# Where a unit of weights begins in its tile: one start per stage and block instead of two

## The chip, the cores and the metric

The kernel runs on one core of a Trainium2 chip. The metric is the device time of one execution in microseconds (us); lower is better. The kernel before was timed twice: 2617.41 and 2624.41 us, median 2620.91 us.

## What is computed

One decoder layer in float32, with 512 rows of 2048 numbers. Cut to its products:

```python
q_a, k_a, v_a, q_b, k_b, v_b = split(h @ w_in)            # 2048 -> 4608 columns
o_a = swa_sink_attention(q_a, k_a, v_a, sinks)            # 16 heads, window of 128
o_b = stick_breaking_attention(q_b, k_b, v_b)             # 16 heads
h = layer_norm(ALPHA * h + concat(rms(o_a), rms(o_b)) @ w_o)
h = layer_norm(ALPHA * h + memory_cross_attention(h, mem, w_q, w_kv, w_o_mem))
gate, up = split(h @ w_gate_up)                           # 2048 -> 2 x 5632
h = layer_norm(ALPHA * h + (silu(gate) * up) @ w_down)    # 5632 -> 2048
```

## The kernel before

All weights go through TensorE in units of 128 x 1024 float32 numbers. For each unit SyncE loads the raw numbers into a staging tile (`stage`, line 137), ScalarE casts them to a rounded half `hi` (line 131), and VectorE subtracts that from the raw numbers and writes the rest as a second half `lo` (line 132). Activations are held as such pairs too. A product is then three matmuls (`mm3`, lines 157 to 162, and its forms for the feed-forward part, `product` at line 1074 and `product_turned` at line 1085): hi by hi, hi by lo, lo by hi. Each matmul comes with a weight load of 128 columns, since TensorE holds one operand (the stationary one, 128 x 128) and streams the other (the moving one) in 256 or 512 columns.

Both halves of a unit lie in one tile of 2048 + 16 float32 numbers, 8256 bytes per partition (`weight_pair`, line 143). Three such tiles are used in turn. The argument `shift` says at which number of the tile `hi` begins; `lo` begins 1024 numbers later. Before the change there are two values: 0, and `SHIFT` = 16 numbers, that is 64 bytes. The three tiles and all tiles of activations that the products below read begin 32 bytes past a multiple of 128 bytes. So a unit with shift 0 begins 32 bytes past such a multiple, and one with shift 16 begins 96 bytes past it.

The stages in order of time. Counts are matmuls on units of weights:

| units | what | operand that the weights are | columns streamed | matmuls | shift before |
|---|---|---|---|---|---|
| wvb | values of B | moving | 512 | 384 | 0 |
| wva | values of A | moving | 256 | 192 | 0 |
| wkb, wqb, wka, wqa | projections, between pieces of attention | stationary | 512 | not touched | 0 |
| wmv, wmk | values and keys of the memory | stationary | 256 | 768 each | 16 |
| wo, wmo | output projections | moving | 512 | 768, 384 | 0 |
| wmq | queries of the memory, turned into `kq` | stationary | 256 | 768 | 16 |
| wvo | mixed values | moving | 512 | 384 | 0 |
| wge | parts of gate and up ahead of time | stationary | 256 | 576 | 16 |
| gu3, gu0, gu4, gu1, gu5, gu2, gu6 to gu10 | gate and up, in this order | stationary | 256 | 672 each; gu0, gu1, gu2: 480 | 16 |
| dn0_0, dn0_1, dn1_0, dn1_1, dn2_0, dn2_1 | down | moving | 512 | 336 each; dn2_0, dn2_1: 252 | 0 |

The order on TensorE and SyncE is written out by hand; the other engines take their work in an order that a scheduler sets when the program is built. TensorE waits for a unit's `hi` (from ScalarE) and `lo` (from VectorE), and ScalarE waits for TensorE to be done with the tile three units earlier. In the gate and up blocks VectorE also adds two raw tiles for most units (line 620), which with line 132 makes two passes over 1024 numbers a unit.

In traces a unit has its name without numbers that count buffers: `gu7w`, `wmk_0w`, `dn_0w` (all units of dn0_0, dn1_0 and dn2_0), `wva2w`.

Of the kernel before, what the change touches and what calls it, by code (L numbers as in the profile page):

```python
# [64 lines left out]
def layer(ctx, tc, io, out):  # L65
# [72 lines left out]
    def stage(src, name):  # L138
        st = pw.tile([P, 1024], F32, tag="ws", name=f"{name}s")
        nc.sync.dma_start(st, src)  # L140
        return st

    def weight_pair(name, shift=0):

        pair_pools.append(pair_pools.pop(0))
        w = pair_pools[-1].tile([P, 2048 + SHIFT], F32R, tag="w", name=f"{name}w")
        return [w[:, k * 1024 + shift:][:, :1024] for k in range(2)]

    def unit(src, name, shift=0):
        st = stage(src, name)  # L150
        hi, lo = weight_pair(name, shift)
        latest[0] = split(hi, lo, st).ins
        return hi, lo
# [57 lines left out]
    for nb in range(2):  # L211
        acc = four_banks(nb, f"v{nb}")
        for u in range(8):
            if nb == 0 and u == 0:
                st, ws = pw.tile([P, 2, 512], F32, tag="ws", name="x0s"), pw.tile([P, 1024], F32, tag="ws", name="wvb0s")
                w = weight_pair("wvb0")
                for c in range(2):
                    nc.sync.dma_start(st[:, c], io["xT"][0][:, cs(c, 512)])
                    nc.sync.dma_start(ws[:, cs(c, 512)], io["w_vb"][0, 0][:, cs(c, 512)])
                for c in range(2):  # L220
                    split(*xc(c), st[:, c])
                    split(*at(w, ALL, cs(c, 512)), ws[:, cs(c, 512)])
            elif nb == 0:
                st = stage(io["xT"][u], f"x{u}").rearrange("p (c n) -> p c n", c=2)
                for c in range(2):
                    split(*xc(2 * u + c), st[:, c])
            if nb > 0 or u > 0:
                w = unit(io["w_vb"][nb, u], f"wvb{nb}_{u}")
            for c in range(2):
                for t in range(NT):  # L230
                    mm3(acc[t], at(xc(2 * u + c), ALL, cs(t, P)), at(w, ALL, cs(c, 512)),
                        u == 0 and c == 0, u == 7 and c == 1)
        for t in range(NT):
            split(vb[t][0][:, cs(nb, 512)], vb[t][1][:, cs(nb, 512)], acc[t])
    load_consts()
    acc = four_banks(0, "va")
    for u in range(4):
        w = unit(io["w_va"][u], f"wva{u}")
# [354 lines left out]
    def steps(name, src, groups, partial, last):  # L593
# [19 lines left out]
        def hilo(src_):  # L613
            hi, lo = weight_pair(name, shift)
            latest[0] = split(hi, lo, src_).ins
            latest[1] = casts[-1]
            return hi, lo
# [93 lines left out]
    def next_unit():  # L711
        while len(ahead) <= AHEAD:
            w = next(source, None)
            if w is None:
                break
            ahead.append(w)
        return ahead.pop(0)
# [18 lines left out]
    for nb in range(4):  # L736
        acc = four_banks(nb, f"wo{nb}")
        for u in range(8):
            w = next_unit()
# [107 lines left out]
    for h in range(4):  # L847
        for nb in range(4):
            acc = ps_z(f"vo{nb}_{h}")
            for u in range(2):  # L850
                w = next_unit()
# [176 lines left out]
    for half in range(2):  # L1028
        for pair in range(2):
            acc = four_banks(1 - pair, f"pvo{half}_{pair}")  # L1030
            spare[:] = [ps_tr, ps_av, ps_lin, ps_lin] if pair == 1 else [ps_z1]
            for h in range(4):
                for j in range(2):
                    nb = 2 * pair + j
                    w = next_unit()
# [324 lines left out]
    for i, kind in enumerate(block_kinds):  # L1360
# [15 lines left out]
        for place in order:  # L1376
            name, role = PRODUCTS[place]
# [109 lines left out]
```

## Time and profile before

| | |
|---|---|
| two timed runs | 2617.41 and 2624.41 us, median 2620.91 us |
| the profiled execution | 2628.31 us |
| its span, first to last instruction | 2626.4 us |
| TensorE matmul busy | 97% of the span |
| TensorE weight loads busy | 87% |
| VectorE, ScalarE, GpSimd busy | 73%, 45%, 7% |
| granted TensorE clock, mean | 0.993 |

PE is TensorE's matmuls, PEld its weight loads, DVE is VectorE, ACT is ScalarE, POOL is GpSimd. Matmuls overlap: a row gives one matmul from its start to its end, which is longer than the distance to the next one's start. That distance is read from a stretch of time and the count of matmuls in it. A count includes those that reach over the edges of the stretch, about two at these lengths.

### The profile page before, as it was taken

The numbers are of one execution on the slowest core, as the hardware profiler recorded it, in microseconds if no ns is written. First come the engines' busy times: TensorE is split into PE (matmuls) and PEld (weight loads), VectorE is DVE, ScalarE is ACT, GpSimd is POOL, SyncE is SP. The second block draws the span as 40 slices with busy tenths as digits, with TensorE's granted clock in tenths as the row PEclk, the third lists the DMA queues.
The fourth block names the chain that finished last, engine by engine and source line by source line (L and its number), as shares of the span: only waits on it lengthen the run. The fifth ranks groups of instructions, "written<-read, shape, count | busy, mean of one in ns | idle before, by whom it ended". The sixth has DMA issues, their size and how long they took to land.

```text
span 2626.4 us, 40562 instructions
## 1 busy us (share of the span) xinstructions
PE 2555.2 (97%) x16544; PEld 2294.9 (87%) x16544; DVE 1907.0 (73%) x2183; ACT 1189.8 (45%) x1572; POOL 186.9 (7%) x325
## 2 busy tenths in 40 slices
PE   9999999999999999999999999999999998999996
PEld 7887777799988889988999999999999997878874
DVE  4258888997632474447788888888887778777797
ACT  4246566665521254334554444544455443333332
POOL 0001101110000000000100101010111001000001
PEclk9999999999999999999999999999999999999998
DMA  5322222245752484235755656464555577787765
GB/s 184 102 82 72 77 73 74 76 166 184 236 185 99 157 274 152 97 113 200 247 186 197 230 210 221 178 245 139 187 209 190 196 264 281 264 328 273 255 257 127
DMA packets 134746, 478.52 MB, mean 182 GB/s; under 512 B 16544, under 2 KB 16928, under 8 KB 133920
## 3 DMA queue, kind: packets, MB, share of 16 engines
q1 hardware_dynamic: 110160, 389.94, 42.2%
q0 software_dynamic: 24400, 86.00, 9.0%
q8 instruction: 129, 2.11, 0.3%
q14 instruction: 57, 0.47, 0.1%
HBM read 403.00 MB, written 72.88 MB: 181 GB/s over the span
## 4 chain that ended last, share of the span: by engine, by line
issue 41%; PE 40%; DVE 9%; DMA 4%; ACT 3%; POOL 3%; SPq 0%; POOLq 0%; DVEq 0%; ACTq 0%
PE zz L1085 16%; PE zz L1074 11%; DVE a L365 1%; POOL f_d L1194 1%; DMA dn_0s<-in_w_dn 1%; PE mvp L160 1%; PE mvp L162 1%; PE mvp L161 1%; DVE a L367 1%; PE pjqa L160 1%; PE pjqa L162 1%; PE pjqa L161 1%; DMA s3r<-f_d 1%; DVE dn_0w L132 0%; DVE pbl L132 0%
## 5 line engine op out<-in xcount | busy, mean ns | idle before, releaser
L131 ACT CAST dn_0w<-dn_0a 128x1024 fp32r<-128x1024 f32 x44 | 46.0, 1052 | 74.3 <-PE zz L1074 45.8
L131 ACT CAST dn_1w<-dn_1a 128x1024 fp32r<-128x1024 f32 x44 | 46.4, 1054 | 68.8 <-PE zz L1074 67.1
L132 DVE TENSOR_TENSOR dn_0w<-dn_0a,dn_0w 128x1024 fp32r<-128x1024 f32 x44 | 53.3, 1221 | 21.1 <-ACT dn_0w L131 21.0
L132 DVE TENSOR_TENSOR dn_1w<-dn_1a,dn_1w 128x1024 fp32r<-128x1024 f32 x44 | 53.5, 1219 | 20.8 <-ACT dn_1w L131 20.8
L365 DVE TENSOR_TENSOR_SCAN a<-ones,nl 128x128 f32<-128x128 f32 (+3 forms) x64 | 49.8, 811 | 9.1 <-POOL nl L362 8.9
L1194 POOL DMA_DIRECT2D f_d<-fha x33 | 17.8, 540 | 395.8 <-ACT fha L131 395.3
L131 ACT CAST fhs<-f 128x512 fp32r<-128x512 f32 x44 | 27.3, 621 | 37.1 <-DVE f L1003 26.0
L362 POOL TENSOR_SCALAR_AFFINE_SELECT nl<-nl 128x256 f32<-128x256 f32 x32 | 19.6, 613 | 338.0 <-DVE nl L361 322.1
L131 ACT CAST dn_0w<-dn_0b 128x1024 fp32r<-128x1024 f32 x22 | 23.2, 1054 | 45.1 <-PE zz L1074 39.6
L131 ACT CAST dn_1w<-dn_1b 128x1024 fp32r<-128x1024 f32 x22 | 23.2, 1055 | 37.9 <-PE zz L1074 31.8
L368 ACT ACTIVATE a<-a 128x256 f32<-128x256 f32 (+3 forms) x32 | 23.6, 739 | 36.8 <-DVE a L367 36.3
L440 ACT ACTIVATE sa<-sa,nm 128x256 f32<-128x256 f32 x64 | 31.9, 501 | 13.7 <-DVE nm L438 13.7
L1074 PE MATMUL zz<-dn_0w,s4h 128*128 128x512 f32 x88 | 29.3, 412 | 7.8 <-DVE dn_0w L132 7.8
L160 PE MATMUL mvp<-mh,wmv_1w 128*128 128x256 f32 x128 | 36.8, 288 | 0.0
L160 PE MATMUL mvp<-mh,wmv_0w 128*128 128x256 f32 x128 | 36.5, 285 | 0.0
L162 PE MATMUL mkp<-mh,wmk_0w 128*128 128x256 f32 x128 | 36.0, 282 | 0.0
L160 PE MATMUL mkp<-mh,wmk_1w 128*128 128x256 f32 x128 | 36.0, 282 | 0.0
L161 PE MATMUL mkp<-ml,wmk_1w 128*128 128x256 f32 x128 | 36.0, 282 | 0.0
L162 PE MATMUL mkp<-mh,wmk_1w 128*128 128x256 f32 x128 | 36.0, 281 | 0.0
L161 PE MATMUL mkp<-ml,wmk_0w 128*128 128x256 f32 x128 | 36.0, 281 | 0.0
L160 PE MATMUL mkp<-mh,wmk_0w 128*128 128x256 f32 x128 | 36.0, 281 | 0.0
L162 PE MATMUL mvp<-mh,wmv_0w 128*128 128x256 f32 x128 | 35.9, 280 | 0.0
(2259 smaller groups left out, 10086.1 us busy)
## 6 DMA issues: line engine op xcount, KB each, us to landing
dn_0s<-in_w_dn SPq DMA_DIRECT2D x33, 512.0 KB, 10.1
dn_1s<-in_w_dn SPq DMA_DIRECT2D x30, 512.0 KB, 6.9
f_d<-fhs POOLq DMA_DIRECT2D x44, 256.0 KB, 2.7
f_d<-fls POOLq DMA_DIRECT2D x44, 256.0 KB, 3.0
f_d<-fha POOLq DMA_DIRECT2D x33, 256.0 KB, 5.5
f_d<-fla POOLq DMA_DIRECT2D x33, 256.0 KB, 5.0
wmv_0s<-in_w_mv SPq DMA_DIRECT2D x16, 512.0 KB, 3.3
wmv_1s<-in_w_mv SPq DMA_DIRECT2D x16, 512.0 KB, 3.2
```

Of the source, the lines that this page charges most:

```text
L131: casts[:] = [nc.scalar.copy(hi, src).ins]
L132: return nc.vector.tensor_tensor(lo, src, f32(hi), op=ALU.subtract)
L160: nc.tensor.matmul(acc, lh, rh, start=first, stop=False)
L161: nc.tensor.matmul(acc, lh, rl, start=False, stop=False)
L162: nc.tensor.matmul(acc, ll, rh, start=False, stop=last)
L365: nc.vector.tensor_tensor_scan(a[:, h, :nk][:, ::-1], ones.to_broadcast([P, nk]), nlt[:, h, :nk][:, ::-1], 0.0, op0=ALU.mult, op1=ALU.add)
L367: nc.vector.tensor_tensor(a[:, :, :nk], zz, a[:, :, :nk], op=ALU.subtract)
L368: nc.scalar.activation(a[:, :, :nk], a[:, :, :nk], AF.Exp)
L440: nc.scalar.activation(s4[:, i], s4[:, i], AF.Exp, bias=nm[:, i:i + 1], accum_out=rs[:, i:i + 1])
L1074: nc.tensor.matmul(acc[:, t], l[:, cs(t, P)], r, start=first and c == 0 and i == 0, stop=last and c == 1 and i == 2, skip_group_check=True)
L1085: nc.tensor.matmul(z[:, j], l[:, cs(j, P)], r, start=first and c == 0 and i == 0 and j % 2 == 0, stop=last and c == 1 and i == 2, skip_gro ...
L1194: nc.gpsimd.dma_start(f_d[chunk, F_BLOCKS[name], k][:, slot * 256:slot * 256 + 512], f32(v))
```

## The change

A table in `weight_pair` sets the start by the unit's name, in float32 numbers of 4 bytes; a name that starts with `w` is matched by its beginning, the others in full. Starts are then 0, 8, 16, 24, 32, 40, 48 or 64 bytes. Units without an entry (the projections wkb, wqb, wka, wqa) keep shift 0. Units of wge and gu3 keep 64 bytes, dn2_1 keeps 0. The sizes and places of all tiles, the instructions, their order on each engine and what they wait for are the same as before.

```diff
+    SHIFTS = {"wvb": 8, "wva": 8, "wo": 4, "wmo": 12, "wvo": 2, "wmq": 4, "wmv": 8, "wmk": 12, "wge": 16,
+              "gu3": 16, "gu0": 2, "gu4": 8, "gu1": 12, "gu5": 4, "gu2": 6, "gu6": 10, "gu7": 8, "gu8": 12, "gu9": 4,
+              "gu10": 2, "dn0_0": 8, "dn0_1": 4, "dn1_0": 12, "dn1_1": 2, "dn2_0": 16, "dn2_1": 0}
+
     def weight_pair(name, shift=0):
 
+        for key, value in SHIFTS.items():
+            if name == key or (key[0] == "w" and name.startswith(key)):
+                shift = value
         pair_pools.append(pair_pools.pop(0))
         w = pair_pools[-1].tile([P, 2048 + SHIFT], F32R, tag="w", name=f"{name}w")
         return [w[:, k * 1024 + shift:][:, :1024] for k in range(2)]
```

## Rows read from the trace of the kernel before

**Rows 1.** The page: busy time of each engine, share of the span, instructions.
```profile
PE 2555.2 (97%) x16544; PEld 2294.9 (87%) x16544; DVE 1907.0 (73%) x2183; ACT 1189.8 (45%) x1572; POOL 186.9 (7%) x325
```

**Rows 2.** The page: the chain that ended last, by engine.
```profile
issue 41%; PE 40%; DVE 9%; DMA 4%; ACT 3%; POOL 3%; SPq 0%; POOLq 0%; DVEq 0%; ACTq 0%
```

**Rows 3.** TensorE by stretch: us, length, busy (matmuls), granted clock, DMA share, GB/s.
```profile
98.00:118.00 20.00, 20.00 (x169) 1.00 0.30 104
735.00:900.00 165.00, 165.00 (x729) 1.00 0.37 132
1400.00:1420.00 20.00, 20.00 (x179) 1.00 0.53 188
1900.00:1920.00 20.00, 20.00 (x172) 1.00 0.42 135
```

**Rows 4.** Weight loads: wva, 98 to 118 us; gu3, 1400 to 1420; gu7, 1900 to 1920.
```profile
L160 PEld LDWEIGHTS vaa<-wva2w,xh 128*128 128x128 f32 x8 | 1.5, 192 | 0.0
...
L1085 PEld LDWEIGHTS zz<-a12h,gu3w 128*128 128x128 f32 x64 | 9.7, 188 | 0.0
...
L1085 PEld LDWEIGHTS zz<-a12h,gu7w 128*128 128x128 f32 x57 | 8.8, 190 | 0.0
```

**Rows 5.** Matmuls: wkb at 120 to 140 us, wo at 735 to 900.
```profile
L160 PE MATMUL pjkb<-xh,wkb_1w 128*128 128x512 f32 x8 | 3.1, 390 | 0.0
...
L160 PE MATMUL wo0a<-wo_6w,mixh 128*128 128x512 f32 x4 | 1.6, 390 | 0.0
```

**Rows 6.** Weight loads of gu2 at 1732 to 1736 us, then at 1742 to 1746.
```profile
L1085 PEld LDWEIGHTS zz<-s4l,gu2w 128*128 128x128 f32 x9 | 1.7, 188 | 0.0
...
L1085 PEld LDWEIGHTS zz<-s3l,gu2w 128*128 128x128 f32 x12 | 2.3, 192 | 0.0
```

**Rows 7.** TensorE's timeline in gu2: start, length, what, idle time before it.
```profile
1738.66 0.28 PE L1085 MATMUL zz<-s4h,gu2w 128*128 128x256 f32 x1
1739.42 0.36 PE L1085 MATMUL zz<-s3h,gu2w 128*128 128x256 f32 x1 [0.48 <-DVE f L136]
1739.62 0.28 PE L1085 MATMUL zz<-s3l,gu2w 128*128 128x256 f32 x1
1740.46 0.50 PE L1085 MATMUL zz<-s3h,gu2w 128*128 128x256 f32 x2 [0.57 <-DVE gu2w L132]
```

**Rows 8.** TensorE by stretch: wmk, gu4, gu5, gu6, gu8, gu10.
```profile
645.00:725.00 80.00, 80.00 (x682) 1.00 0.74 239
...
1486.00:1562.00 76.00, 75.22 (x660) 1.00 0.54 200
...
1626.00:1702.00 76.00, 75.08 (x656) 1.00 0.54 197
...
1765.00:1840.00 75.00, 75.00 (x638) 1.00 0.47 167
...
1925.00:2000.00 75.00, 75.00 (x639) 1.00 0.46 167
...
2085.00:2158.00 73.00, 73.00 (x623) 1.00 0.74 258
```

**Rows 9.** Matmuls of wmv over the whole span and of wmq at 1005 to 1176 us.
```profile
L161 PE MATMUL mvp<-ml,wmv_1w 128*128 128x256 f32 x128 | 35.8, 280 | 0.0
...
L161 PE MATMUL kq<-ktl,wmq_2w 128*128 128x256 f32 x32 | 9.0, 280 | 0.0
...
L161 PE MATMUL kq<-ktl,wmq_5w 128*128 128x256 f32 x32 | 8.9, 278 | 0.0
```

**Rows 10.** TensorE's waits: us in total, times, longest.
```profile
PE zz L1085 <- DVE gu2w L132: 3.1, 4, 1.8
PE zz L1085 <- DVE gu0w L132: 2.6, 3, 1.4
...
PE zz L1085 <- ACT gu0w L131: 1.5, 1, 1.5
```

**Rows 11.** A stretch of gu0: length, then busy of PE, PEld, DVE, ACT, POOL.
```profile
1434.00:1484.00 50.00, 45.90 (x383) 45.10 (x383) 41.72 (x42) 21.45 (x24) 6.48 (x12) 0.97 0.57 191
```

**Rows 12.** Casts and subtractions of units that begin at 64 bytes (gu10) and at 0 (dn).
```profile
L132 DVE TENSOR_TENSOR dn_0w<-dn_0a,dn_0w 128x1024 fp32r<-128x1024 f32 x44 | 53.3, 1221 | 21.1 <-ACT dn_0w L131 21.0
...
L132 DVE TENSOR_TENSOR gu10w<-gu10a,gu10w 128x1024 fp32r<-128x1024 f32 x16 | 19.5, 1222 | 7.6 <-ACT gu10w L131 7.6
...
L131 ACT CAST dn_0w<-dn_0a 128x1024 fp32r<-128x1024 f32 x44 | 46.0, 1052 | 74.3 <-PE zz L1074 45.8 <-DVE dn_0a L620 25.3 <-PE zz L1085 1.8
...
L131 ACT CAST gu10w<-gu10a 128x1024 fp32r<-128x1024 f32 x16 | 16.8, 1048 | 14.7 <-PE zz L1085 11.2 <-issue 2.5 <-ACT gu10w L131 0.9
```

## The prediction

> **What bounds the kernel now.** I read the engines' busy shares first. TensorE's matmuls cover 97% of the span and its weight loads 87%; VectorE has 73% [rows 1]. The chain that ended last says the same: most of it is TensorE and its issue, 9% is VectorE [rows 2]. So the time is a count of matmuls times the distance from one start to the next, and that distance is where a new start address can act. I read it next, in stretches where PE is busy throughout at the full granted clock [rows 3]. Two matmuls reach over the edges, so 20.00 us is divided by 177 in gu3: 113.0 ns. In gu7 it is 20.00 / 170 = 117.6 ns, in wva 20.00 / 167 = 119.8 ns, each for 256 columns. In wo, with 512 columns, it is 165.00 / 727 = 227.0 ns. Three levels for the same 256 columns is the point of this case; I call them A (113.0), B (117.6) and C (119.8).
>
> The weight loads tell the levels apart too [rows 4]: 188 ns each at A, 192 at C, and at B a mean of 190 in the group shown. wva is the only stage with 256 columns whose unit begins at 0 bytes, and it is at C throughout. The stages that begin at 64 bytes are at A or at B, and address alone does not choose between these two: in gu2 every load takes 188 ns until 1736 us, and after two waits of 0.48 and 0.57 us one load in three takes 192 [rows 6, 7]. From there on gu6, gu8 and gu10 stay at B (75.00 / 636 = 117.9 ns in gu6), as wmk does (80.00 / 680 = 117.6), while gu4 and gu5 were at A once their waits are taken off (75.22 / 658 = 114.3, 75.08 / 654 = 114.8) [rows 8]. B is thus a rhythm between loads and matmuls that a wait can start. wmv and wmq lie between: their matmuls take 278 to 280 ns [rows 9]. A matmul's length in rows is its distance plus some 163 ns (390 against 227.0), so these are at 115 to 117 ns; I use 116.5 for wmv and 116 for wmq.
>
> With 512 columns the row is 390 ns whether the weights are the moving operand (wo) or the stationary one (wkb) [rows 5], and no stage begins anywhere but at 0 bytes.
>
> **The change part by part.** No instruction, wait or tile is added, removed or moved. Each unit is written by ScalarE and VectorE and read by TensorE at another start. So there are three questions.
>
> Writing: casts take 1048 ns into a start of 64 bytes and 1052 into 0, subtractions 1222 and 1221 [rows 12]. I cost the new starts at nothing. Cover where it fails is thin only in gu0 to gu2, where VectorE is busy for 41.72 of 50 us [rows 11].
>
> Stationary units with 256 columns. The trace has only the two ends, 0 bytes (C) and 64 bytes (A or B). For a start between them I take the end that it is nearer to; 32 bytes is halfway, and I put it with 64, since the unit then no longer begins in the same 64-byte piece as before.
>
> - Starts of 8, 16 and 24 bytes go to C. gu0: 480 x 6.8 ns = 3.3 us. gu5: 672 x 6.8 = 4.6. gu2, at A until about 1740 us, some 62% of its time, and then at B: 480 x (0.62 x 6.8 + 0.38 x 2.2 = 5.05) = 2.4. gu9 and gu10, from B: 1344 x 2.2 = 3.0. wmq: 768 x 3.8 = 2.9. Together 16.2 us lost. In gu0 and gu2 TensorE already waits for ScalarE and VectorE, 2.6 + 1.5 and 3.1 us [rows 10], and a slower TensorE waits less. Half of their 5.7 us is hidden so: 2.8.
> - Starts of 32, 40 and 48 bytes stay at A or B. gu1 and gu4 keep A. wmk (768), gu6, gu7, gu8 (2016) could go from B to A at 4.6 ns each, 3.5 + 9.3 us, and wmv (768 x 3.5) 2.7: together 15.5. The rhythm may start again after any wait, so I take half: 7.7 gained.
>
> Moving units. [...] I take no change except at 32 bytes, where the unit begins on a multiple of 64 bytes: there half a step for wvb and dn0_0 (720 x 3.4 = 2.4 us) and for wva (192 x 3.4 = 0.7) is gained.
>
> The sum is 16.2 - 2.8 - 7.7 - 3.1 = +2.6 us. The profiled execution took 2628.3 us, so it would take 2630.9. It lies 7.4 us above the median of the two runs, 2620.9; carried over, the forecast is 2623.5, rounded to 2624 us.
>
> Both ends: if every changed stationary unit goes to C, the loss is 16.2 + gu4 4.6 + gu1 3.3 + wmk and gu6 to gu8 (2784 x 2.2) 6.1 + wmv 2.5 = 32.7 us. If all go to A, the gain is 15.5 + wmq 2.3 + gu9 and gu10 6.2 + gu2 0.8 = 24.8, and a step of 6.8 ns for the moving units from 32 bytes on (1692 with 512 columns, 192 with 256) adds 12.8: 37.6 us.
>
> [...] The rows show that the distance depends on where the stationary operand begins or on how loads and matmuls fall together: 113.0, 117.6 and 119.8 ns at one clock [rows 3]. [...]
>
> **The rivals.**
>
> 1. The 64-byte start was the good one and every other start is like 0: all changed stationary units at C, +32.7 us, 2654 us. For it: wva at C from start to end. Against it: one stage is little to generalise from, and there the weights are the moving operand.
> 2. The start does not matter; the rhythm alone does, and waits set it. Then the time is 2621 us, give or take the 7 us between the runs. For it: gu2 changes level at a fixed address [rows 6, 7]. Against: wva never shows A.
> 3. The distance falls where the two operands no longer meet: 37.6 us gained, 2583 us. [...] Against: no row is under 113 ns.
> [...]
>
> **How the numbers follow.** The forecast's mixture has 0.42, rival 1 0.15, rival 2 0.20, rival 3 0.15, of which half beyond 2% (52.4 us), rival 4 0.08. A measurement can tell about 2% from no change here. So faster by more than 2%: 0.08; slower by more: 0.09 (rival 4 and a little of rival 1); within 2%: 0.83. The range goes from rival 3's first figure, 2583, to rival 1's with 8 us for starts that are worse than C, 2662.
>
> **What would show it.** Right: stretches of gu0, gu5, gu9 and gu10 at 120 ns with loads of 192, gu4 and gu1 at 113, gu6 to gu8 at 113 or 118, 227 in wo and in dn0_1; casts and subtractions unchanged. Wrong: any stretch with 256 columns under 113 or over 121 ns, 512 columns away from 227 in more than the units at 32 bytes, or a subtraction longer than 1225 ns.

## The result, and the profile after

| | us |
|---|---|
| before, two timed runs | 2617.41 and 2624.41, median 2620.91 |
| after, two timed runs | 2654.54 and 2661.15, median 2657.85 |
| ratio after to before | 1.0127, 95% interval 1.0096 to 1.0157 |
| profiled execution of after | 2661.15, span 2659.4 |

The change costs 1.3%. That is inside 2% of no change and inside the range, but not the +2.6 us that I had summed: it is 33.3 us by the ratio and 36.9 us by the medians.

The busy shares and the chain that ended last, of the page of after, beside [rows 1, 2]:

```profile
PE 2592.1 (97%) x16544; PEld 2314.6 (87%) x16544; DVE 1909.0 (72%) x2183; ACT 1191.1 (45%) x1572; POOL 186.9 (7%) x325
...
issue 41%; PE 41%; DVE 8%; DMA 4%; ACT 3%; POOL 2%; SPq 0%; POOLq 0%; DVEq 0%; ACTq 0%
```

All instruction counts are the same, and so are VectorE and ScalarE to 0.1%. Only TensorE is busy longer, 2592.1 against 2555.2 us: 36.9 us, and the span is 33.0 us longer. The loss is TensorE's own, not a wait.

Where, by stretches. These are TensorE's windows in after (us, length, busy and matmuls, granted clock, DMA share, GB/s), in order wvb, wva, wmk, wo, gu4, gu5, gu6, gu8, gu10, dn0_1, dn1_1:

```profile
20.00:95.00 75.00, 75.00 (x323) 1.00 0.43 140
98.00:118.00 20.00, 20.00 (x173) 1.00 0.25 80
655.00:735.00 80.00, 79.25 (x672) 1.00 0.73 232
740.00:905.00 165.00, 165.00 (x714) 1.00 0.38 133
...
1505.00:1575.00 70.00, 70.00 (x594) 1.00 0.49 177
1645.00:1715.00 70.00, 70.00 (x593) 1.00 0.49 172
1790.00:1860.00 70.00, 70.00 (x590) 1.00 0.42 147
1945.00:2020.00 75.00, 75.00 (x610) 1.00 0.42 154
2110.00:2140.00 30.00, 30.00 (x260) 1.00 0.86 312
2280.00:2345.00 65.00, 65.00 (x282) 1.00 0.71 250
...
2440.00:2510.00 70.00, 70.00 (x302) 1.00 0.67 235
```

Each is read as before: busy time by matmuls less two. One matmul more or less moves the two short stretches (wva, gu10) by 0.5 to 0.7 ns. The granted clock is 1.00 in all, as in the stretches of before, so the clock explains nothing.

| stage | start, bytes | columns | before, ns | after, ns |
|---|---|---|---|---|
| wvb | 0, now 32 | 512 | 227 (all such stages) | 75.00 / 321 = 233.6 |
| wo | 0, now 16 | 512 | 227.0 [rows 3] | 165.00 / 712 = 231.7 |
| dn0_1 | 0, now 16 | 512 | 227 | 65.00 / 280 = 232.1 |
| dn1_1 | 0, now 8 | 512 | 227 | 70.00 / 300 = 233.3 |
| wva | 0, now 32 | 256 | 119.8 [rows 3] | 20.00 / 171 = 117.0 |
| wmk | 64, now 48 | 256 | 117.6 [rows 8] | 79.25 / 670 = 118.3 |
| gu4 | 64, now 32 | 256 | 114.3 [rows 8] | 70.00 / 592 = 118.2 |
| gu5 | 64, now 16 | 256 | 114.8 [rows 8] | 70.00 / 591 = 118.4 |
| gu6 | 64, now 40 | 256 | 117.9 [rows 8] | 70.00 / 588 = 119.0 |
| gu8 | 64, now 48 | 256 | 117.7 [rows 8] | 75.00 / 608 = 123.4 |
| gu10 | 64, now 8 | 256 | 117.6 [rows 8] | 30.00 / 258 = 116.3 |

For the down units of before, which [rows 3] does not show, this is its stretch of dn1_0 and dn1_1, 100.00 / 441 = 226.8 ns:

```profile
2380.00:2480.00 100.00, 100.00 (x443) 1.00 0.69 243
```

Two things stand out. The matmuls with moving weights and 512 columns, most of which I had left alone, lose some 5 to 7 ns each. And with stationary weights no changed stage is at the best level of before, 113 ns, and most sit at 118 or above.

### The profile page after: what moved, and what is told of

Same layout as the page of the kernel before. It is cut to its first block, busy times and chain, and to the rows that moved or that the text cites. A ratio compares the mean times of both kernels' runs of the same rounds, so it can differ in the third digit from the quotient of the medians.

```text
span 2659.4 us, 40562 instructions
## 1 busy us (share of the span) xinstructions
PE 2592.1 (97%) x16544; PEld 2314.6 (87%) x16544; DVE 1909.0 (72%) x2183; ACT 1191.1 (45%) x1572; POOL 186.9 (7%) x325
## 4 chain that ended last, share of the span: by engine, by line
issue 41%; PE 41%; DVE 8%; DMA 4%; ACT 3%; POOL 2%; SPq 0%; POOLq 0%; DVEq 0%; ACTq 0%
PE zz L1092 15%; PE zz L1081 12%; DMA dn_0s<-in_w_dn 2%; DVE a L372 1%; POOL f_d L1201 1%; PE mvp L167 1%; PE mvp L169 1%; PE mvp L168 1%; PE pjqa L167 1%; PE pjqa L168 1%; PE pjqa L169 1%; DVE a L374 1%; ACT nl L367 0%; ACT nl L365 0%; PE pjkb L167 0%
## 5 line engine op out<-in xcount | busy, mean ns | idle before, releaser
L167 PE MATMUL mvp<-mh,wmv_1w 128*128 128x256 f32 x128 | 36.9, 288 | 0.0
L627 DVE TENSOR_TENSOR dn_0a<-dn_0a,dn_0s 128x1024 f32<-128x1024 f32 x22 | 26.6, 1218 | 14.2 <-DMA dn_0s<-in_w_dn 14.2
L168 PE MATMUL mvp<-ml,wmv_0w 128*128 128x256 f32 x128 | 36.0, 281 | 0.0
L167 PE MATMUL mkp<-mh,wmk_1w 128*128 128x256 f32 x128 | 36.0, 281 | 0.0
L168 PE MATMUL mvp<-ml,wmv_1w 128*128 128x256 f32 x128 | 36.0, 281 | 0.0
```

Of the source, the lines that this page charges most:

```text
L167: nc.tensor.matmul(acc, lh, rh, start=first, stop=False)
L168: nc.tensor.matmul(acc, lh, rl, start=False, stop=False)
L627: nc.vector.tensor_tensor(dst, dst, x, op=ALU.add)
```

## The experiments

The question was first whether the two halves of the loss are separate, and then what a start has to be measured against: the chip's memory (absolute place), pieces of 64 or 128 bytes of it, or the other operand of the same matmul. "Before" in each comparison was run on the same chip; 17 runs of it stand beside the first four kernels here, 23 beside the next three and the odd starts, one beside the last.

**Only the moving units.** The table keeps wvb, wva, wo, wmo, wvo and the down units; all others begin where they did before.

```diff
+    SHIFTS = {"wvb": 8, "wva": 8, "wo": 4, "wmo": 12, "wvo": 2,
+              "dn0_0": 8, "dn0_1": 4, "dn1_0": 12, "dn1_1": 2, "dn2_0": 16, "dn2_1": 0}
```

> The table keeps only the entries of units that are the moving operand (wvb, wva, wo, wmo, wvo, dn); all stationary units begin at 64 bytes as before. In the changed kernel's profile the distance of 512-column matmuls went from 227 ns to about 232 (16 bytes) and 233 (8, 32 and 48 bytes). Theory 1, the time lies in these matmuls by themselves: about 18 us over before, some 2639 us, with wo at 232 ns and wvb at 233 in its profile. Theory 2, what was seen there is the stationary part handing on its delays: within 5 us of before, 2621 us.

Measured: 2636.3 us (six runs) against 2621.1, ratio 1.0059 (1.0040 to 1.0077). So 0.59% of 2620.9, 15.5 us, comes from here. TensorE's windows in this run, wo and gu8:

```profile
740.00:900.00 160.00, 160.00 (x692) 1.00 0.35 125
1930.00:2000.00 70.00, 70.00 (x620) 1.00 0.47 178
```

wo is at 160.00 / 690 = 231.9 ns, as in after, and gu8, whose start is the old one, at 70.00 / 618 = 113.3: level A, where the profiled execution of before had it at B.

**Only the stationary units.**

```diff
+    SHIFTS = {"wmq": 4, "wmv": 8, "wmk": 12, "wge": 16,
+              "gu3": 16, "gu0": 2, "gu4": 8, "gu1": 12, "gu5": 4, "gu2": 6, "gu6": 10, "gu7": 8, "gu8": 12, "gu9": 4,
+              "gu10": 2}
```

> The table keeps only the entries of units that are the stationary operand (wmv, wmk, wmq, wge, gu); moving units begin at 0 bytes as before. Theory 1, each start has its own distance (8 bytes 115.7 ns, 16 and 32 bytes 118.3, 24 and 40 bytes 119.2, 48 bytes 118 to 123, 64 bytes 113 or 118): about 12 to 18 us over before, some 2633 to 2639 us, and with the other half alone it adds up to the 37 us of the whole change within 8 us. Theory 2, all starts other than 64 bytes are like 0 bytes (120 ns): gu0 and gu10 at 120 ns and some 2650 us.

Measured: 2639.97 us (six runs), ratio 1.0068 (1.0053 to 1.0084), 17.8 us. The two parts add to 0.59 + 0.68 = 1.27%, the whole change. wo in this run, and gu8 at 48 bytes:

```profile
740.00:900.00 160.00, 160.00 (x707) 1.00 0.36 126
1930.00:2000.00 70.00, 70.00 (x596) 1.00 0.43 162
```

wo is back at 160.00 / 705 = 227.0. gu8 is at 70.00 / 594 = 117.8, not 123.4 as in after with the same start: a start does not fix a stage's level alone.

**Everything 32 bytes later.** A tile of 8 numbers is put behind the constants and ahead of all other tiles; every tile of weights and of activations moves by 32 bytes.

```diff
+    pad = const.tile([P, 8], F32, name="pad")
+    nc.gpsimd.memset(pad, 0.0)
```

> The kernel before with one more constant tile of 32 bytes ahead of all others, so that every tile of activations and of weights lies 32 bytes later; units begin at 0 and 64 bytes in their tiles as before. Every unit with shift 0 now begins on a multiple of 64 bytes, and so does every activation. Theory 1, what counts is how far apart the starts of the two operands lie, modulo 64 or 128 bytes: 227 ns with 512 columns, 113 or 118 with 256, and the time of before within 8 us (2613 to 2629 us). Theory 2, what counts is where the weights begin by themselves, and a multiple of 64 bytes costs 233 ns as wvb does in the changed kernel: about 5000 matmuls with 512 columns at 6.6 ns more, some 2654 us. Theory 3, an operand on a multiple of 64 bytes needs one piece of 64 bytes less: faster, 220 ns with 512 columns, some 2590 us.

Measured: 2620.06 us (12 runs), ratio 1.0000 (0.9987 to 1.0013). wo, and a stretch of gu8 and some gu9, which run at A in this execution (70.00 / 618):

```profile
740.00:900.00 160.00, 160.00 (x707) 1.00 0.34 121
1930.00:2000.00 70.00, 70.00 (x620) 1.00 0.47 169
```

A move of both operands together by 32 bytes does not matter to 0.13%, while a shift of the weights alone by the same 32 bytes takes wvb from 227 to 233.6 ns. What matters is the start relative to the activations'. In before the tiles of activations and of weights all begin 32 bytes past a multiple of 256 bytes in the program's addresses, so the shift is itself the distance between the two operands' starts, modulo 256.

**A map of larger starts, up to 192 bytes.** The tile grows by 128 bytes to hold them, and the small tile `mv` has two buffers in place of four.

```diff
+    SHIFTS = {"wvb": 16, "wva": 16, "wo": 32, "wmo": 24, "wvo": 14, "wmq": 40, "wmv": 26, "wmk": 2, "wge": 16,
+              "gu3": 16, "gu0": 48, "gu4": 14, "gu1": 36, "gu5": 18, "gu2": 46, "gu6": 20, "gu7": 24, "gu8": 28, "gu9": 30,
+              "gu10": 32, "dn0_0": 6, "dn0_1": 10, "dn1_0": 20, "dn1_1": 30, "dn2_0": 48, "dn2_1": 40}
...
-        w = pair_pools[-1].tile([P, 2048 + SHIFT], F32R, tag="w", name=f"{name}w")
+        w = pair_pools[-1].tile([P, 2048 + 48], F32R, tag="w", name=f"{name}w")
...
-        mv = sm.tile([P, 4], F32, tag="mv", name=f"{name}mv{t}", bufs=4)
+        mv = sm.tile([P, 4], F32, tag="mv", name=f"{name}mv{t}", bufs=2)
```

> A map: the weight tiles are 128 bytes longer, so that starts up to 192 bytes can be read, and the table gives each stage a start that was not yet seen (in bytes: wvb and wva 64, wo 128, wmo 96, wvo 56; wmq 160, wmv 104, wmk 8; gu3 64, gu0 192, gu4 56, gu1 144, gu5 72, gu2 184, gu6 80, gu7 96, gu8 112, gu9 120, gu10 128; dn0_0 24, dn0_1 40, dn1_0 80, dn1_1 120, dn2_0 192, dn2_1 160). Theory 1, two operands hinder each other by the distance of their starts modulo 128 bytes: wo at 128 bytes back at 227 ns, gu10 at 128 bytes at 120 ns as 0 bytes had, gu0 at 192 bytes like 64 (113 or 118), wmk at 8 bytes like gu10 in the changed kernel (115.7). Theory 2, the distance counts modulo 64 bytes: wvb at 64 and wo at 128 bytes both 227 ns. Theory 3, any start but the old two costs a matmul with 512 columns 5 to 7 ns: wo 232 to 233 ns.

Measured: one run, 2648.61 us. TensorE's windows: wvb (64 bytes), wmk (8), wo (128), gu10 (128):

```profile
20.00:95.00 75.00, 75.00 (x327) 1.00 0.40 139
645.00:725.00 80.00, 80.00 (x689) 1.00 0.71 234
740.00:900.00 160.00, 160.00 (x694) 1.00 0.36 125
...
2105.00:2170.00 65.00, 65.00 (x549) 1.00 0.70 246
```

wvb takes 75.00 / 325 = 230.8, wmk 80.00 / 687 = 116.4, wo 160.00 / 692 = 231.2, gu10 65.00 / 547 = 118.8. For wo a start of 128 bytes is not as good as 0, so 64 or 128 bytes is no period. The reading is clouded: the larger tile also moved one weight tile in three by 128 bytes against the activations. Taken apart by the distance modulo 256 in the program's addresses, 504 of wo's matmuls at 128 follow each other at a mean of 233.2 ns and 264 at 0 at 227.4, close to the old 227. Hence the next two kernels.

**The weights alone 128, then 256 bytes later.** A tile of 32 (then 64) numbers lies between the activations' pools and the weights'; the starts in the tiles are those of before. The staging tiles and small tiles behind the weights move along; of what TensorE reads in wo, only the weights move.

```diff
+    gap_pool = ctx.enter_context(tc.tile_pool(name="gp", bufs=1))
...
+    gap = gap_pool.tile([P, 32], F32, name="gap")
+    nc.gpsimd.memset(gap, 0.0)
```

> The kernel before with one more tile of 128 bytes between the activations' tiles and the weight tiles. Units begin at 0 and 64 bytes in their tiles as before, and each operand keeps its place modulo 128 bytes; only the two are 128 bytes further apart. Theory 1, the distance of the two starts counts modulo 256 bytes (0 is the good one for 512 columns): wo from 227 to about 233 ns, all 512-column stages together 5 us and more per thousand matmuls, and 256 columns at about 118 to 119 ns; some 35 us over before, 2656 us. Theory 2, it counts modulo 64 or 128 bytes: the time of before, 2621 us within 8.

> As weights128, but with 256 bytes between. Theory 1, modulo 256 bytes: 227 ns with 512 columns, 113 or 118 with 256, 120 in wva, and the time of before, 2621 us within 8. Theory 2, any other place of the weight tiles costs, be it how far: some 2650 us as in the changed kernel. Theory 3, the period is 512 bytes: 512-column stages at about 233 ns.

Measured: 128 bytes 2647.86 us (four runs) against 2619.84, ratio 1.0110 (1.0089 to 1.0132); 256 bytes 2619.45 (ten runs), ratio 1.0009 (0.9994 to 1.0024). TensorE's windows of wo and of 1930 to 2000 us (mostly gu8) at 128 bytes:

```profile
740.00:900.00 160.00, 160.00 (x687) 1.00 0.35 124
1930.00:2000.00 70.00, 70.00 (x597) 1.00 0.52 191
```

and the same two at 256 bytes:

```profile
740.00:900.00 160.00, 160.00 (x708) 1.00 0.36 128
1930.00:2000.00 70.00, 70.00 (x620) 1.00 0.47 168
```

wo takes 160.00 / 685 = 233.6 ns at 128 and 160.00 / 706 = 226.6 at 256. With no number of the table touched, moving one operand by 128 bytes costs almost as much as the whole change (1.1% against 1.3%), and moving it by 256 costs nothing. The staging tiles are not the cause: in the map all of wo's matmuls ran beside the same staging tiles, and there too those at a distance of 0 were at 227.4 and those at 128 at 233.2. Where the weights stream in 512 columns, the distance of the two operands' starts counts modulo 256 bytes; that is the finding of this study.

Two readings limit it. The second stretch takes 117.6 and 113.3 ns, but these are B and A, which the same placement has in different executions, so it does not tell 128 from 256. At 128 bytes gu3 is at A, 40.00 / 353 = 113.3:

```profile
1380.00:1420.00 40.00, 40.00 (x355) 1.00 0.20 67
```

And the projections, which stream 512 columns of activations against stationary weights, hardly notice the move. TensorE in wkb and the start of wqb, in before and at 128 bytes:

```profile
121.00:131.00 10.00, 10.00 (x45) 1.00 0.31 107
121.00:131.00 10.00, 10.00 (x45) 1.00 0.30 107
```

Both are at 10.00 / 43 = 232.6 ns. Averaged from one matmul row's start to the next over all of wkb, wqb, wka and wqa (gaps over 280 ns left out), a stage is at 230.5 to 231.6 ns at a distance of 0 and at 232.2 to 232.6 at 128. So a distance of 0 alone does not give 227 ns; why these stages are slower at it is open.

**All stationary units at 8 bytes, moving units at 0.**

```diff
+    SHIFTS = {"wmq": 2, "wmv": 2, "wmk": 2, "wge": 2, "gu": 2}
...
+            if name.startswith(key):
```

> Of the table only one rule is left: every stationary unit that began at 64 bytes (wmv, wmk, wmq, wge, all gu) begins at 8 bytes, and moving units at 0 as before. Theory 1, 8 bytes has one steady distance of 115.7 ns (as gu0 and gu10 had), where 64 bytes changes between 113.3 and 117.8: all these stages at 115 to 117 ns in the profile, the time of before within 6 us, and runs closer together. Theory 2, gu0 and gu10 had their 115.7 ns from what went before them: stages at 118 to 120 ns and 2640 us.

Measured: 2618.81 us (12 runs), ratio 0.9996 (0.9983 to 1.0009). TensorE in three stretches, nearly all of gu7, gu8 and gu9:

```profile
1850.00:1920.00 70.00, 70.00 (x608) 1.00 0.44 159
1930.00:2000.00 70.00, 70.00 (x608) 1.00 0.44 160
2005.00:2075.00 70.00, 70.00 (x608) 1.00 0.44 158
```

Each is at 70.00 / 606 = 115.5 ns: between A and B, without either. The 12 runs lie within 5.6 us (2616.42 to 2621.97), the 23 of before beside it within 18.9 us (2612.38 to 2631.29). Before can be a little faster or slower, as its stages fall on A or B. That this makes the spread is not shown run by run, but two traced executions fit it: by the distances of all stages, the one of the kernel with everything 32 bytes later (2615.58 us) should be some 9 us shorter than that of before (2628.31), and it is 12.7 us shorter. The total is that of before, 1.3% under after's.

**Odd multiples of 4 bytes.** Most units begin at an odd multiple of 4 bytes, 4 to 60; gu0 is at 8, wva at 64, and wo and three of the down blocks are at 0.

```diff
+    SHIFTS = {"wvb": 1, "wva": 16, "wo": 0, "wmo": 15, "wvo": 3, "wmq": 1, "wmv": 3, "wmk": 15, "wge": 1,
+              "gu3": 1, "gu0": 2, "gu4": 3, "gu1": 1, "gu5": 15, "gu2": 15, "gu6": 13, "gu7": 1, "gu8": 3, "gu9": 5,
+              "gu10": 15, "dn0_0": 3, "dn0_1": 5, "dn1_0": 0, "dn1_1": 7, "dn2_0": 0, "dn2_1": 0}
```

> A second map, with starts that are odd multiples of 4 bytes (wvb 4, wmo 60, wvo 12, wmq 4, wmv 12, wmk 60, wge, gu3, gu1 and gu7 4, gu4 and gu8 12, gu9 20, gu6 52, gu5, gu2 and gu10 60, gu0 8; dn0_0 12, dn0_1 20, dn1_1 28; wo and the other dn at 0, wva at 64). Theory 1, pieces of 8 bytes count: 4 bytes like 0 or 8 bytes (512 columns 227 or 233 ns; 256 columns 120 or 115.7), 60 bytes like 56 or 64. Theory 2, an odd start splits pairs of numbers and is worse than any even one: over 121 ns with 256 columns, over 235 with 512. A start with 256 columns steadily at 113 ns would be the one to build a faster version on.

Measured: one run, 2650.18 us. TensorE's windows: wvb (4 bytes), gu8 (12), gu7 (4), gu9 (20), gu10 (60), dn0_1 (20), dn1_1 (28):

```profile
20.00:95.00 75.00, 75.00 (x318) 1.00 0.42 139
...
1940.00:2010.00 70.00, 70.00 (x603) 1.00 0.43 160
1860.00:1930.00 70.00, 70.00 (x594) 1.00 0.43 160
2025.00:2090.00 65.00, 65.00 (x544) 1.00 0.37 133
2105.00:2170.00 65.00, 65.00 (x546) 1.00 0.69 238
2275.00:2340.00 65.00, 65.00 (x273) 1.00 0.67 234
2435.00:2500.00 65.00, 65.00 (x288) 1.00 0.67 235
```

With 512 columns: 75.00 / 316 = 237.3 at 4 bytes, 65.00 / 271 = 239.9 at 20, but 65.00 / 286 = 227.3 at 28. With 256 columns: 116.5 at 12, 118.2 at 4, 119.9 at 20, 119.5 at 60. So the worst starts are among these, and one of them, 28, is as good as 0. From one row's start to the next, wmo at 60 bytes is almost as good, 227.5 ns, and wvo at 12 is at 229.0. None is better than 227 or 113.

**The two halves at different starts.** `hi` and `lo` of a unit get starts of their own, so that a matmul and the next see different distances.

```diff
+    SHIFTS = {"wmq": (2, 2), "wmv": (2, 16), "wmk": (0, 16), "wge": (16, 2),
+              "gu3": (2, 16), "gu0": (16, 16), "gu4": (16, 2), "gu1": (0, 16), "gu5": (0, 2), "gu2": (16, 0), "gu6": (16, 8),
...
+        late = shifts[0] > shifts[1]
+        return [w[:, (k != late) * 1024 + shifts[k]:][:, :1024] for k in range(2)]
```

> A third map: the two halves of a unit begin at different distances. In bytes, the rounded half then the rest: gu3 and wmv 8 and 64, gu4 and wge 64 and 8, gu1 and wmk 0 and 64, gu5 0 and 8, gu2 64 and 0, gu6 64 and 32, gu7 32 and 64, gu8 12 and 64, gu9 64 and 12, gu10 8 and 0, gu0 64 and 64, wmq 8 and 8; moving: wva 64 and 8, wmo 0 and 28, wvo 28 and 0, dn0_0 0 and 64, dn0_1 64 and 0, dn1_0 0 and 60, dn1_1 60 and 0, dn2_0 28 and 60. Theory 1, each matmul has the price of its own pair of starts, whatever the one before had: a group of three is the weighted mean, 2:1 for the rounded half where the weights are stationary (gu3 (2 x 115.7 + 113.3) / 3 = 114.9 to 116.4 ns; gu4 114.1 to 117.1). Theory 2, the rhythm of 117.8 ns lives on three equal distances in a row, so a pair with 64 and 8 bytes stays at 114 to 115 ns steadily, and all 256-column stages set so would give 5 to 10 us. Theory 3, a change of distance from one matmul to the next costs by itself: 118 ns and more everywhere.

Measured: one run, 2639.32 us, beside one of before at 2628.81 on that chip. TensorE's windows: gu3 (8 and 64 bytes), gu4 (64 and 8), gu6 (64 and 32):

```profile
1360.00:1420.00 60.00, 59.48 (x514) 1.00 0.32 114
1500.00:1560.00 60.00, 60.00 (x504) 1.00 0.39 141
1775.00:1840.00 65.00, 65.00 (x555) 1.00 0.38 136
```

116.2, 119.5 and 117.5 ns: no mixture is at A, and gu4's is worse than 8 bytes throughout (115.5). Changing the distance from one matmul to the next does not keep the good rhythm going. Theory 3, that such a change costs by itself, falls with gu3 for 256 columns (116.2, not 118 and more). With 512 columns it holds: from one row's start to the next, wmo with its halves at 0 and 28 bytes takes 230.4 ns and dn1_0 with 0 and 60 takes 234.8, where 0, 28 and 60 throughout take 226.8, 227.2 and 227.5. So the distance within one matmul does not set its price alone; what its neighbour's is counts too. One run beside one run tells nothing about the total.

## Why the prediction's range held and its working failed

The time fell inside the range, 4 us below its upper end, and within 2% as the chances said. The working failed: two of its four terms had the wrong sign, and a third was more than twice too large. That the range held is luck in part. Its upper end has every changed stationary unit at C, 8 us on top, and nothing for the moving units, where one step of 6.8 ns (A to C) on each would have been 3516 x 6.8 = 23.9 us more; the moving units did lose, and the stationary ones lost less than C. Two of the prediction's own signs of being wrong showed: 512 columns away from 227 ns at 8 and 16 bytes, and gu8 over 121 ns.

- **Writing costs nothing: right.** Casts and subtractions are unchanged beside [rows 12]. In after, of gu10 (8 bytes) and dn_0 over the span:

```profile
L131 ACT CAST dn_0w<-dn_0a 128x1024 fp32r<-128x1024 f32 x44 | 45.8, 1048 | 75.9 <-PE zz L1081 44.5
...
L132 DVE TENSOR_TENSOR dn_0w<-dn_0a,dn_0w 128x1024 fp32r<-128x1024 f32 x44 | 53.3, 1220 | 20.5 <-ACT dn_0w L131 20.4
...
L132 DVE TENSOR_TENSOR gu10w<-gu10a,gu10w 128x1024 fp32r<-128x1024 f32 x16 | 19.5, 1221 | 7.2 <-ACT gu10w L131 7.2
```

- **"Moving units: I take no change except at 32 bytes", -3.1 us: this step failed.** Measured alone, the moving units cost +15.5 us, and 32 bytes, where I had a gain of half a step, 3.4 ns, is among the worst of the table: no run shows that gain with 512 columns, and wvb lost 6.6 ns there (233.6 against 227). One step of 6.8 ns (A to C) bounds the loss for the table's starts: the rows of the table above give 4.7 to 6.6. For other starts it does not (12.9 ns at 20 bytes). That no stage with 512 columns began anywhere but at 0 bytes was a reason for a wide range and not for zero. Only wva, with 256 columns, gained at 32 bytes, 2 to 3 ns on 192 matmuls: the one part of that term that came true.
- **"Starts of 32, 40 and 48 bytes stay at A or B", -7.7 us: this step failed.** No such stage gained; they are at 118.2, 119.0, 118.3 and 123.4 ns, and gu4 lost its A. The sum of the stationary terms was 16.2 - 2.8 - 7.7 = +5.7 us; measured alone it is +17.8. The rule behind this step and the next, that a start is like the end that it is nearer to, is wrong: 40 and 48 bytes are nearer to 64 and at 118.3 to 123.4 ns, not at A, and 8 is nearer to 0 and not at C. With 512 columns too 28 bytes is like 0 and 20 is not.
- **"Starts of 8, 16 and 24 bytes go to C", +16.2 us: the loss was there, but more than twice too large.** gu5 (16 bytes) went from 114.8 to 118.4, a little under C, and gu2 (24 bytes) came near it, 119.2 from one row's start to the next. gu10 (8 bytes) went the other way, from 117.6 to 116.3, and 8 bytes proved the steady level of 115.5 in its own experiment. By the distances of the two profiled executions the six stages together lost some 7 us.
- **Half of the loss in gu0 and gu2 hidden by waits, -2.8 us: the number came out, the half is not shown.** TensorE's waits in after, beside [rows 10]:

```profile
PE zz L1092 <- DVE gu0w L132: 2.6, 4, 0.8
...
PE zz L1092 <- DVE gu2w L132: 1.9, 5, 0.6
```

  gu0's fell from 4.1 us (its wait for ScalarE is gone) to 2.6 and gu2's from 3.1 to 1.9, together 2.7. But the loss in the two was some 3 us by the distances, not 5.7, and before's waits were long in that execution: in the kernel with everything 32 bytes later, whose starts in these stages are the old ones, they are 3.0 and 2.4 us, 1.8 less without any change of start.
- **The carrying over from one profiled execution.** I read before's levels off one execution. Which stages fall on A is not the same in each: gu8 was at B there and at A in three of the runs above with the same start and distance. That execution, at 2628.3, stands near the slow end of before's 23 runs above, so its level B was no fixed thing to gain from.

Of the rivals, the first (all changed stationary units at C, 2654 us) has the nearest time, but not for its reason: it left the moving units alone, and they are almost half of the loss (15.5 of 33.3 us). The second, that the start does not matter, falls with 1.0127. The third, a distance that falls, falls too: no stage of any run is under 113 ns with 256 columns or under 226 with 512. So no run shows a ground for the half of its chance that I put beyond 2%. None shows one for the 0.08 of rival 4, slower by more than 2%, either: with 512 columns a start of 8 bytes costs 6.3 ns (dn1_1, 233.3 against 227.0) and the dearest start read, 20 bytes, costs 12.9 (239.9 against 227.0), while a loss of 2% is 52.4 us, 14.9 ns on each of the 3516 matmuls.

That the two operands' places matter to each other is measured: with the weights moved by 128 bytes against the activations, wo's distance goes from 227 to 233.6 ns and the kernel is 1.1% slower.

What stays open: why 0, 28 and 60 bytes are best with 512 columns and 64 with 256; why the projections are at 231 ns at a distance of 0; why two good distances in turn cost more than either; by what the two operands' places act on each other, since no run shows how they are read; and what starts rhythm B, which was seen after waits [rows 7] but not started on purpose.

## What to carry to other kernels

Read the distance from one matmul's start to the next by stage, from a stretch without waits, before asking what engine to relieve: at a busy share of 97% the placement of tiles alone cost 1.1% here (the weights 128 bytes later) and 1.3% (the change), and for the change neither the busy share (97% before and after) nor TensorE's waits (52.3 us in all before, 48.8 after) show it. None of the placements tried here was faster than the one of before. Where float32 operands stream with a weight load for each matmul, the best found here is a distance of 0 modulo 256 bytes, the same for every matmul, where the weights stream in 512 columns (226.6 to 227.0 ns), and 8 bytes (115.5 ns) or 64 (113.3 or some 117.8) where they are held and 256 columns stream. Check the addresses after any change to pool sizes, since a tile of 128 bytes put in between cost 1.1% here. And a stage's level read off one execution is a sample (gu8 at 117.7 and at 113.3 ns with the same start and distance): look at a second one before pricing a gain from it.

## What the runs showed of the hardware that was not expected

- With the weights as the moving operand, the distance of the two operands' starts modulo 256 bytes changes the spacing: 512 columns take 226.6 to 227.0 ns at 0, 227.3 at 28, 231 to 234 at 8, 16, 32 and 128, 237.3 at 4 and 239.9 at 20. Two good distances in turn cost 230.4 to 234.8.
- With stationary weights, 256 columns and 64 bytes there are two rhythms, 113.3 and some 117.8 ns, and the same stage can have either in different executions; with 8 bytes throughout gu7, gu8 and gu9 were all at one, 115.5 ns, and the kernel's runs spread over 5.6 us and not 18.9.
- The weight load's own row hardly tells the level apart where I had read it so: gu8 in after, at 123.4 ns, has loads of 190 ns, as gu7 had in before at 117.6 [rows 4]:

```profile
L1092 PEld LDWEIGHTS zz<-s1h,gu8w 128*128 128x128 f32 x64 | 10.1, 190 | 0.0
```
